# A transformer block on one Trainium2 core: the remainder of every second gate and up block comes from an accumulating transfer

## The chip, the core and the metric

The kernel runs on one of the eight cores of a Trainium2 chip. A core has a matrix engine (TensorE, PE in the profile; its weight loads are listed as PEld), VectorE (DVE), ScalarE (ACT), GpSimd (POOL) and SyncE (SP), which run their own instruction streams and wait for one another by semaphores, and 16 DMA engines that move data between memory (HBM) and the on-chip buffer (SBUF) or inside SBUF. TensorE adds up in PSUM, a separate memory of 8 banks per partition. The metric is the time of one execution on the device, in microseconds (us).

## The reference

One encoder layer for 256 tokens of width 2048, in float32: a layer norm, a wide projection, two kinds of recurrent mixing (gated linear recurrence and retention), an output projection with a residual and a second layer norm, and then the feed-forward part, which is where the change lies:

```
h = layer_norm(DEEPNORM_ALPHA * h + mix, ln1_g[layer], ln1_b[layer])
ff = (jax.nn.silu(h @ w_gate[layer]) * (h @ w_up[layer])) @ w_down[layer]
h = layer_norm(DEEPNORM_ALPHA * h + ff, ln2_g[layer], ln2_b[layer])
```

The gate and up weights are 2048 x 5632 each, the down weight is 5632 x 2048.

## The kernel before

**Products in split form.** TensorE reads float32 operands in a rounded format (fp32r in the profile). To keep accuracy the kernel splits every operand a into a rounded part, hi, and the remainder, lo = a - hi, and adds up the products hi*hi, hi*lo and lo*hi.

**The weight stream.** All weights come as blocks of 128 partitions x 2048 float32 values (1024 KB). `fetch` (L56 to L61) issues the load of one block from SyncE into a tile `raw`, of which there are three (`rawp`, bufs=3). `split_parts` (L71 to L76) then makes the two parts: ScalarE copies `raw` into `whi` with rounding (L75), and VectorE subtracts, `wlo = raw - whi` (L76). There are three pairs of `whi` and `wlo` (`splitp`, bufs=3). So block n can be split once TensorE is done with block n-3, and block n can be loaded once block n-3 has been split. SyncE issues the loads in the order of the blocks, and waits at each until its `raw` tile is free.

**The gate and up stage.** `hidden` (L828) makes two tiles of 128 hidden features, of gate (u = 0) and then of up (u = 1). Each needs one weight block, so that a call uses four blocks, in the order (u, j) = (0,0), (0,1), (1,0), (1,1). `both` (L830) multiplies a block: for each of 16 chunks of the contraction, one product of `whi` with the hi and lo parts of all tokens (512 columns, L838) and one of `wlo` with the hi part (256 columns, L837, or L841 for the first chunk). For the first chunk the product with `whi` comes first. After a block, ScalarE copies one half of the PSUM bank (L850) and VectorE adds the other to it (L851). PSUM has four such banks for these products (`psp`, bufs=4). After two blocks ScalarE and VectorE work on the pair (L855 and L856, or L858, L860 and L861). The stage is in two pieces, hidden tiles 4 to 23 and 24 to 43, with 40 blocks each, and each piece is followed by products with the down weights, whose blocks are split in the same way. The first four hidden tiles are made by another function, which the change leaves alone.

**What sets the order.** Each engine runs its instructions in the order that the tile scheduler wrote when the kernel was built; a waiting instruction holds back all that come behind it on its engine. A tile of a pool is handed out again when its last reader is done.

Of the kernel before, what the change touches and what calls it, by code (L numbers as in the profile page):

```python
# [31 lines left out]

# column offsets of the packed per-feature parameters
C_LB, C_HG, C_RG, C_RB, C_IG, C_IB, C_1G, C_1B = 0, 16, 24, 32, 40, 56, 72, 88
# [4 lines left out]
def encoder_kernel(ctx: ExitStack, tc: tile.TileContext, x, meta, par, rows, w_in, w_out,  # L39
# [13 lines left out]

# [1 line left out]
    def fetch(src, parts=1):  # L55
# [24 lines left out]

# [1 line left out]
    soon, steps = [], deque()  # L82
# [18 lines left out]
    def token_group(blocks, operand, order, evac, split_of=None, halve=False):  # L101
        """[256 tokens] x [512 columns]; a block has 4 chunks of the contraction; order: (token tile, block)

        halve: the second tile goes by column halves at the end; evac(i, ps, half)
        """
        ps = [psp.tile([P, 512], F32, name="pp") for _ in range(2)]
        ws, left, seen = {}, [sum(1 for t, _ in order if t == i) for i in range(2)], [0, 0]
        for i, g in order:
            if g not in ws:
                ws[g] = split_of(g) if split_of else load_block(blocks[g])  # L110
            whi, wlo = ws[g]
            left[i] -= 1
            if halve and i:
                if left[i]:
                    continue
                n = len(ws)
                for half in range(2):
                    ph = psp.tile([P, 512], F32, name="pp")
                    for k in range(4 * n):
                        a_hi, a_lo = operand(i, k)  # L120
                        c = (k % 4) * 512 + half * 256
                        for m, (a, w) in enumerate(((a_hi, 0), (a_hi, 1), (a_lo, 0))):
                            nc.tensor.matmul(ph[:, :256], a, ws[k // 4][w][:, c:c + 256],  # L123
                                             start=(k == 0 and m == 0), stop=(k == 4 * n - 1 and m == 2))
                    evac(i, ph[:, :256], half)
                continue
            for j in range(4):
                k = 4 * g + j
                a_hi, a_lo = operand(i, k)
                for m, (a, w) in enumerate(((a_hi, whi), (a_hi, wlo), (a_lo, whi))):  # L130
                    nc.tensor.matmul(ps[i], a, w[:, j * 512:(j + 1) * 512],  # L131
                                     start=(seen[i] == 0), stop=(left[i] == 0 and j == 3 and m == 2))
                    seen[i] = 1
                if j % 2:
                    tick()
            if left[i] == 0:
                if halve:
                    evac(i, ps[i][:, :256], 0)
                    evac(i, ps[i][:, 256:], 1)
                else:  # L140
                    evac(i, ps[i])
# [7 lines left out]

# [1 line left out]
    prm = cpool.tile([P, NPAR], F32, name="prm")  # L151
# [33 lines left out]

    # lower bounds: softmax over the two rows, first one
    lb = cpool.tile([P, 8], F32, name="lb")
# [14 lines left out]

# [1 line left out]
    def stats_of(xt, st, np_, c0, c1):  # L204
# [3 lines left out]
    def moments(mom, rstd, shift, st, np_):  # L208
        """mean and variance; 1 / deviation; -mean / deviation"""
        nc.vector.bn_aggr(out=mom[:np_], in_=st[:np_])  # L210
        rsqrt(rstd[:np_], mom[:np_, 1:2], 1, np_, LN_EPS)
        nc.vector.tensor_scalar(out=shift[:np_], in0=mom[:np_, 0:1], scalar1=rstd[:np_], scalar2=-1.0,
                                op0=ALU.mult, op1=ALU.mult)
# [4 lines left out]
    def affine_split(pt, pool, cg, cb, c, hs, ls, on_act):  # L218
        """four transposed [P, P] chunks in PSUM -> scaled, shifted, split"""
        fl = pool.tile([P, 4, P], F32, name="fl", tag="w", bufs=6 if pool is not lnp else 3)  # L220
# [86 lines left out]
    def project(n):  # L307
        """weights stationary: [P features, n tokens]"""
        nonlocal nblk
# [13 lines left out]
    def silu_group(order, dst, scale, split_of=None):  # L323
        """silu of 512 columns, token-major"""
        nonlocal nblk
        b0 = nblk
        nblk += 4

        def evac(i, ps):
            sg = qp.tile([P, 512], F32, name="sg", bufs=2)  # L330
            nc.scalar.activation(sg, ps, AF.Sigmoid)
            nc.vector.scalar_tensor_tensor(out=dst[:, i, :], in0=ps, scalar=scale, in1=sg,
                                           op0=ALU.mult, op1=ALU.mult)
        token_group([w_in[b0 + g] for g in range(4)], halves(xhi, xlo), order, evac, split_of)
# [10 lines left out]
    with tc.tile_pool(name="att", bufs=1) as att:  # L345
# [5 lines left out]
        nc.sync.dma_start(dt, dtab)  # L351
        # retention scores by key tile: [256 queries], [128 + 128 queries], [16 keys, 128 queries]
        RS = att.tile([P, 640], F32, name="RS")
# [3 lines left out]
        def values(ps, v, vm, j, o, om):  # L357
            """feature-major [P, T] in PSUM -> token-major, tiles from column o and 16 tokens from column om"""
            vt = att.tile([P, T], F32, name="vt", bufs=2)
# [10 lines left out]

# [1 line left out]
        W = 2 * SEQ + 2 * NM  # L372

        def hgrn(pr, qt, get_g):
# [28 lines left out]

            # Decays to block boundaries, block sizes b = 1, 2, 4, ...: queries hold the decay from the start of
            # their block, keys the decay to the end of theirs, D the decay over a block.
            E = att.tile([P, 3, 4 * 64], F32, name="E")
# [4 lines left out]
            def across(t, b, w, q):  # L411
                """to blocks of 2 b: odd blocks of queries (q) or even blocks of keys take their neighbour's decay"""
                dv = state["d"][:, :w // b].rearrange("p (n two) -> p n two", two=2)
# [17 lines left out]
            def scores():  # L431
                """keys against the three sets of queries in E, 64 of each tile"""
                scs = []
# [8 lines left out]
            def targets(o, b):  # L442
                """the columns of S of odd and even blocks, two tiles"""
                return [S[:, o:o + 2, :].rearrange("p c (n two b) -> p c n two b", two=2, b=b)[:, :, :, x, :]
                        for x in (1, 0)]
# [8 lines left out]
            def prepare(b):  # L454
                """E: queries of the odd blocks of b; of the odd blocks of 2 b; the latter past one more block"""
                n = 2 * SEQ // (4 * b)
# [61 lines left out]
            def cross():  # L518
                # second tile of queries against the first tile of keys
                sx = pss.tile([P, 512], F32, name="sc")  # L520
# [71 lines left out]

# [1 line left out]
        def retention(r):  # L594
# [18 lines left out]
            def scores():  # L613
                # key tiles: positions 0 .. 127, 128 .. 255, 256 .. 271; queries: positions 16 .. 271
                sc = pss.tile([P, 512], F32, name="sc")
# [69 lines left out]

# [1 line left out]
        acc = actp.tile([P, 2, D], F32, name="acc", tag="big", bufs=2)  # L687
# [40 lines left out]

# [1 line left out]
    ffp = ctx.enter_context(tc.tile_pool(name="ffp", bufs=1))  # L730
# [42 lines left out]

# [1 line left out]
    def h_op(i, k):  # L775
# [24 lines left out]
    def first_hidden():  # L800
        """four hidden tiles, tokens stationary, so that the first tile of tokens can go ahead"""
        gate = [None, None]
# [25 lines left out]
    def hidden(f, s):  # L828
        """two hidden tiles, weights stationary, both parts of the tokens moving at once"""
        def both(u, j):  # L830
            hi, lo = load_block(w_gu[2 * f + 2 * u + j])
            hi = hi.rearrange("p (k c) -> p k c", k=KC)
# [91 lines left out]
def _layout(x, meta_tokens, ln_in_g, ln_in_b, hg_lower_bounds, w_in, hg_norm_g, ret_norm_g, ret_norm_b,  # L924
# [14 lines left out]
    def col_blocks(w):  # L939
        """[feature tile][P rows, chunk x P columns]"""  # L940
        w = a(w)[0].reshape(KC, P, -1, P)
        return w.transpose(2, 1, 0, 3).reshape(-1, P, 2048)

    def row_blocks(w, c0, k0, k1):
        """columns c0 .. c0 + 512, chunks k0 .. k1: [block of 4 chunks][P rows, 4 x 512 columns]"""
        w = a(w)[0][k0 * P:k1 * P, c0:c0 + 512].reshape(-1, 4, P, 512)
# [39 lines left out]
```

## Time and profile before

| | |
|---|---|
| time, median of 2 runs | 1308.49 us (1308.13 to 1308.84) |
| span of the profiled execution | 1308.3 us |
| TensorE busy, share of the span | 1281.8 us, 98% |
| VectorE busy | 755.7 us, 58% |
| ScalarE busy | 541.0 us, 41% |
| GpSimd busy | 12.9 us, 1% |
| DMA engines, mean busy share | 51.5% for the transfers that SyncE issues |
| moved | 237.56 MB, 182 GB/s on average |

The span runs from the first to the last instruction of one execution that the hardware profiler recorded; that is the execution's own time here, and it lies between the two timed runs. Busy shares are averages over stages. Matmuls are pipelined, and their ends in the records are modelled, so that a busy TensorE is not one at its peak; where blocks follow each other, the time per block is read from the distance of the ScalarE copies (L850) that each block releases.

### The profile page before, as it was taken

The numbers are of one execution on the slowest core, as the hardware profiler recorded it, in microseconds if no ns is written. First come the engines' busy times: TensorE is split into PE (matmuls) and PEld (weight loads), VectorE is DVE, ScalarE is ACT, GpSimd is POOL, SyncE is SP. The second block draws the span as 40 slices with busy tenths as digits, with TensorE's granted clock in tenths as the row PEclk, the third lists the DMA queues.
The fourth block names the chain that finished last, engine by engine and source line by source line (L and its number), as shares of the span: only waits on it lengthen the run. The fifth ranks groups of instructions, "written<-read, shape, count | busy, mean of one in ns | idle before, by whom it ended". The sixth has DMA issues, their size and how long they took to land.

```text
span 1308.3 us, 17600 instructions
## 1 busy us (share of the span) xinstructions
PE 1281.8 (98%) x7516; PEld 1125.6 (86%) x7516; DVE 755.7 (58%) x872; ACT 541.0 (41%) x570; POOL 12.9 (1%) x24
## 2 busy tenths in 40 slices
PE   6999999999999999999999999999999999999996
PEld 4989999898999988878888888888888888888886
DVE  7764575565557576675555555544445555555555
ACT  7533334343343333573444444433334444443340
POOL 0000000000000000000000000000000000000000
PEclk9999999999999999999999999999999999999998
DMA  6644443454444477555555555555555555555541
GB/s 230 258 150 151 162 146 126 159 182 149 142 160 147 144 278 269 181 212 188 191 193 184 178 187 191 194 193 193 193 193 186 177 188 191 193 183 189 192 176 65
DMA packets 34958, 237.56 MB, mean 182 GB/s; under 512 B 4016, under 2 KB 4656, under 8 KB 6960
## 3 DMA queue, kind: packets, MB, share of 16 engines
q1 hardware_dynamic: 34880, 236.44, 51.5%
q8 instruction: 59, 0.97, 0.3%
q14 instruction: 19, 0.16, 0.0%
HBM read 234.33 MB, written 2.10 MB: 181 GB/s over the span
## 4 chain that ended last, share of the span: by engine, by line
PE 96%; DVE 2%; ACT 1%; DMA 1%; POOL 0%; issue 0%; SPq 0%; POOLq 0%; DVEq 0%
PE pp L131 32%; PE pp L838 23%; PE pp L317 22%; PE pp L837 11%; PE sc L437 1%; PE pp L123 1%; PE pp L841 1%; DVE wlo L76 1%; PE ms L549 1%; PE sc L618 0%; PE ms L546 0%; DMA xt<-in_x_dram 0%; DMA raw<-in_w_down_dram 0%; ACT fl L225 0%; PE sc L535 0%; ACT whi L75 0%
## 5 line engine op out<-in xcount | busy, mean ns | idle before, releaser
L76 DVE TENSOR_TENSOR wlo<-raw,whi 128x2048 fp32r<-128x2048 f32 (+1 forms) x211 | 479.2, 2271 | 324.1 <-ACT whi L75 317.1
L75 ACT CAST whi<-raw 128x2048 fp32r<-128x2048 f32 (+1 forms) x211 | 399.7, 1894 | 246.0 <-PE pp L131 197.4
L838 PE MATMUL pp<-h,whi 128*128 128x512 f32 x1280 | 446.4, 398 | 0.0
L837 PE MATMUL pp<-h,wlo 128*128 128x256 f32 x1200 | 337.4, 281 | 0.0
L838 PEld LDWEIGHTS pp<-h,whi 128*128 128x128 f32 x1280 | 235.4, 188 | 52.4
L837 PEld LDWEIGHTS pp<-h,wlo 128*128 128x128 f32 x1200 | 226.8, 189 | 3.1
L317 PE MATMUL pp<-xhi,whi 128*128 128x272 f32 (+1 forms) x768 | 224.6, 292 | 0.0
L317 PE MATMUL pp<-xlo,whi 128*128 128x272 f32 (+1 forms) x768 | 219.9, 286 | 0.0
L317 PE MATMUL pp<-xhi,wlo 128*128 128x272 f32 (+1 forms) x768 | 219.2, 285 | 0.0
L131 PE MATMUL pp<-whi,t 128*128 128x512 f32 x648 | 199.6, 389 | 0.0
L317 PEld LDWEIGHTS pp<-xhi,whi 128*128 128x128 f32 x768 | 144.6, 188 | 4.2 <-issue 1.7
L317 PEld LDWEIGHTS pp<-xhi,wlo 128*128 128x128 f32 x768 | 144.7, 188 | 0.2
L317 PEld LDWEIGHTS pp<-xlo,whi 128*128 128x128 f32 x768 | 144.6, 188 | 0.0
L131 PEld LDWEIGHTS pp<-whi,t 128*128 128x128 f32 x648 | 121.6, 188 | 25.1
L850 ACT COPY sum<-pp 128x256 f32<-128x256 f32 x80 | 29.8, 373 | 256.3 <-PE pp L838 256.3
L131 PE MATMUL pp<-wlo,t 128*128 128x512 f32 x324 | 126.2, 389 | 0.7 <-DVE wlo L76 0.7
L851 DVE TENSOR_TENSOR sum<-pp,sum 128x256 f32<-128x256 f32 x80 | 34.0, 425 | 100.8 <-ACT sum L850 100.8
L131 PEld LDWEIGHTS pp<-wlo,t 128*128 128x128 f32 x324 | 60.8, 188 | 13.6 <-DVE wlo L76 0.9
L131 PE MATMUL pp<-whi,xhi 128*128 128x512 f32 x128 | 52.3, 411 | 1.9 <-ACT xhi L229 1.9
L131 PE MATMUL pp<-whi,xlo 128*128 128x512 f32 x128 | 51.0, 398 | 0.8 <-DVE xlo L230 0.8
L131 PE MATMUL pp<-wlo,xhi 128*128 128x512 f32 x128 | 51.5, 402 | 0.0
L131 PE MATMUL pp<-whi,mhi 128*128 128x512 f32 x120 | 46.9, 391 | 0.0
(201 smaller groups left out, 1027.5 us busy)
## 6 DMA issues: line engine op xcount, KB each, us to landing
raw<-in_w_gu_dram SPq DMA_DIRECT2D x88, 1024.0 KB, 4.9
raw<-in_w_in_dram SPq DMA_DIRECT2D x62, 1024.0 KB, 4.9
raw<-in_w_down_dram SPq DMA_DIRECT2D x44, 1024.0 KB, 4.9
raw<-in_w_out_dram SPq DMA_DIRECT2D x16, 1024.0 KB, 4.9
gb<-in_rows_dram SPq DMA_DIRECT2D x6, 1024.0 KB, 7.8
raw<-in_w_in_dram SPq DMA_DIRECT2D x4, 512.0 KB, 8.1
acc<-in_x_dram SPq DMA_DIRECT2D x2, 1024.0 KB, 5.9
out_dram<-acc SPq DMA_DIRECT2D x6, 256.0 KB, 2.3
```

Of the source, the lines that this page charges most:

```text
L75: nc.scalar.copy(hi[:, sl], raw[:, sl])
L76: nc.vector.tensor_tensor(out=lo[:, sl], in0=raw[:, sl], in1=hi[:, sl].bitcast(F32), op=ALU.subtract)
L123: nc.tensor.matmul(ph[:, :256], a, ws[k // 4][w][:, c:c + 256], start=(k == 0 and m == 0), stop=(k == 4 * n - 1 and m == 2))
L131: nc.tensor.matmul(ps[i], a, w[:, j * 512:(j + 1) * 512], start=(seen[i] == 0), stop=(left[i] == 0 and j == 3 and m == 2))
L317: nc.tensor.matmul(ps[:, :n], w[:, kc, :], a[:, kc, T - n:], start=(kc == 0 and j == 0), stop=(kc == KC - 1 and j == 2))
L437: nc.tensor.matmul(sc[:, c * 192:(c + 1) * 192], K[:, (o + c) * P:(o + c + 1) * P], E[:, :, (o + c) * 64:(o + c + 1) * 64], start=True, st ...
L549: nc.tensor.matmul(oo, SM[:NM, j * SEQ + i * P:j * SEQ + (i + 1) * P], Vm[:NM, j, :], start=False, stop=True)
L837: nc.tensor.matmul(ps[:, :SEQ], lo[:, kc, :], h[:, kc, 0, :], start=False, stop=False)
L838: nc.tensor.matmul(ps, hi[:, kc, :], h[:, kc].rearrange("p m t -> p (m t)"), start=(kc == 0), stop=(kc == KC - 1))
L841: nc.tensor.matmul(ps[:, :SEQ], lo[:, kc, :], h[:, kc, 0, :], start=False, stop=False)
L850: nc.scalar.copy(t[:, j, :], ps[:, SEQ:])
L851: nc.vector.tensor_tensor(out=t[:, j, :], in0=ps[:, :SEQ], in1=t[:, j, :], op=ALU.add)
```

## The change

In `hidden`, the second block of each pair (j = 1) is loaded by a new function, `load_added`. ScalarE makes the rounded part as before and also writes minus the rounded block into `wlo`; then a transfer that GpSimd issues reads `raw` and adds it onto `wlo` where it lies, so that `wlo` holds the remainder. There are 40 such blocks. Comments are dropped elsewhere, which moves the lines behind by 9; nothing else is different.

```diff
+    def load_added(src):
+
+        raw, _ = fetch(src)
+        hi, lo = new_split()
+        nc.scalar.copy(hi, raw)
+        nc.scalar.activation(lo, raw, AF.Identity, scale=-1.0)
+        nc.gpsimd.dma_start(lo, raw, accum_op=ALU.add)
+        return hi, lo
...
         def both(u, j):
-            hi, lo = load_block(w_gu[2 * f + 2 * u + j])
+            hi, lo = load_added(w_gu[2 * f + 2 * u + j]) if j else load_block(w_gu[2 * f + 2 * u + j])
```

ScalarE in the middle of the gate and up stage before, for two blocks; L850 is the copy out of PSUM, L75 the rounding copy of the block three further on, L855 belongs to the gate:

```order
L850 COPY sum<-pp 128x256
L75 CAST whi<-raw 128x2048
L850 COPY sum<-pp 128x256
L75 CAST whi<-raw 128x2048
L855 ACTIVATE sg<-sum 128x512
```

ScalarE at the same place now, where L859 is the copy out of PSUM, L85 the rounding copy and L86 the negation of a block with j = 1, and L75 the rounding copy of a block with j = 0:

```order
L86 ACTIVATE wlo<-raw 128x2048
L859 COPY sum<-pp 128x256
L85 CAST whi<-raw 128x2048
L859 COPY sum<-pp 128x256
L75 CAST whi<-raw 128x2048
L864 ACTIVATE sg<-sum 128x512
```

One instruction of 2048 columns is added for two blocks, and it stands ahead of the copy out of PSUM that comes when TensorE is done with the block whose buffers it takes.

GpSimd around the stage now; L193 belongs to the layer norms before and after, L87 is the new transfer:

```order
L193 TENSOR_TENSOR lr<-rst,nhalf 128x1 x2
L87 DMA wlo<-raw 128x2048 x40
L193 TENSOR_TENSOR lr<-rst,nhalf 128x1 x2
```

Between the two norms GpSimd had nothing to do before; now it issues the 40 transfers one after the other, in the order of the blocks.

## Rows read from the trace of the kernel before

**Rows 1.** Page, first line and part 1: busy time, share of the span, instructions

```profile
span 1308.3 us, 17600 instructions
...
PE 1281.8 (98%) x7516; PEld 1125.6 (86%) x7516; DVE 755.7 (58%) x872; ACT 541.0 (41%) x570; POOL 12.9 (1%) x24
```

**Rows 2.** Page, part 4: the chain that ended last, by engine

```profile
PE 96%; DVE 2%; ACT 1%; DMA 1%; POOL 0%; issue 0%; SPq 0%; POOLq 0%; DVEq 0%
```

**Rows 3.** Windows, with the stage's second piece last: columns in the first line

```profile
core 0: us, PE busy (x) PEld busy (x) DVE busy (x) ACT busy (x) POOL busy (x), PEclk, DMA share, GB/s
...
40.00:60.00 20.00, 20.00 (x146) 19.23 (x145) 12.33 (x16) 10.61 (x12) 0.00 (x0) 1.00 0.82 326
...
930.00:1157.00 227.00, 227.00 (x1250) 195.95 (x1249) 124.72 (x101) 94.55 (x91) 0.00 (x0) 1.00 0.54 187
```

**Rows 4.** Timeline of ScalarE, 756 to 804 us: start, duration, engine, line, operation

```profile
762.67 1.91 ACT L75 CAST whi<-raw 128x2048 fp32r<-128x2048 f32 x1
...
768.04 0.37 ACT L850 COPY sum<-pp 128x256 f32<-128x256 f32 x1 [2.95 <-PE pp L838]
768.31 1.91 ACT L75 CAST whi<-raw 128x2048 fp32r<-128x2048 f32 x1
773.69 0.37 ACT L850 COPY sum<-pp 128x256 f32<-128x256 f32 x1 [3.47 <-PE pp L838]
...
779.34 0.37 ACT L850 COPY sum<-pp 128x256 f32<-128x256 f32 x1 [2.94 <-PE pp L838]
```

**Rows 5.** Timeline of VectorE, the same stretch

```profile
763.26 0.69 DVE L858 TENSOR_TENSOR sum<-sum 128x512 f32<-128x512 f32 x1
...
770.26 2.29 DVE L76 TENSOR_TENSOR wlo<-raw,whi 128x2048 fp32r<-128x2048 f32 x1 [1.38 <-ACT whi L75]
```

**Rows 6.** Timeline of TensorE's products, 767.1 to 768.1 us

```profile
767.49 0.28 PE L837 MATMUL pp<-h,wlo 128*128 128x256 f32 x1
```

**Rows 7.** Timeline of TensorE's weight loads, 778.8 to 779.5 us

```profile
779.14 0.19 PEld L841 LDWEIGHTS pp<-h,wlo 128*128 128x128 f32 x1
```

**Rows 8.** Groups of ScalarE by line and shape: busy us, mean ns, idle before

```profile
L75 ACT CAST whi<-raw 128x2048 fp32r<-128x2048 f32 x207 | 395.5, 1910 | 245.6 <-PE pp L131 197.4 <-PE pp L317 33.5 <-issue 10.6
...
L251 ACT ACTIVATE xt<-xt,xs,xr 16x2048 f32<-16x2048 f32 x1 | 2.1, 2082 | 0.0
```

**Rows 9.** Page, part 3: DMA queue, packets, MB, share of 16 engines

```profile
q1 hardware_dynamic: 34880, 236.44, 51.5%
```

**Rows 10.** Page, part 6: loads, count, KB each, us from issue to landing

```profile
raw<-in_w_gu_dram SPq DMA_DIRECT2D x88, 1024.0 KB, 4.9
```

**Rows 11.** Line 59, all loads of weight blocks over the whole span

```profile
DMA to landing us min/median/max: 4.7/4.9/11.5
```

**Rows 12.** What SyncE's queue waited for, 575 to 806 us: total, times, longest

```profile
SPq L59 <- DVE wlo L76: 213.3, 42, 6.4
```

**Rows 13.** Groups of GpSimd by line and shape

```profile
L184 POOL TENSOR_TENSOR lr<-rst,nhalf 128x1 f32<-128x1 f32 x4 | 3.4, 840 | 833.2 <-DVE rst L182 833.2
```

**Rows 14.** Windows of the first products, columns as in Rows 3

```profile
16.00:18.00 2.00, 1.47 (x4) 1.20 (x5) 1.79 (x4) 2.00 (x6) 0.13 (x1) 0.74 0.91 324
18.00:20.00 2.00, 2.00 (x6) 1.54 (x5) 1.54 (x4) 2.00 (x6) 0.42 (x1) 0.50 1.04 430
```

**Rows 15.** Timeline of TensorE at the start, products of 512 columns

```profile
16.53 0.50 PE L131 MATMUL pp<-whi,xlo 128*128 128x512 f32 x1 [0.78 <-DVE xlo L230]
...
18.07 0.63 PE L131 MATMUL pp<-whi,xhi 128*128 128x512 f32 x1
18.49 0.63 PE L131 MATMUL pp<-wlo,xhi 128*128 128x512 f32 x1
...
23.21 0.39 PE L131 MATMUL pp<-whi,xhi 128*128 128x512 f32 x1
23.44 0.40 PE L131 MATMUL pp<-wlo,xhi 128*128 128x512 f32 x1
```

## The prediction

> **What bounds the kernel now.** I read the page's busy times first, then the chain that ended last, then windows of the gate and up stage, then its timeline engine by engine. TensorE is busy for 98% of the span [rows 1], and 96% of the chain that ended last is TensorE's own [rows 2]. In the stage's second piece it is busy for all of 227 us, at full clock, while VectorE works 124.72 us, ScalarE 94.55 us, GpSimd not at all, and the DMA engines have a busy share of 0.54 [rows 3]. So the engine that the change relieves is not the one that sets the time; the question is only whether the new way to the remainder is quick enough.
>
> How quick that is, the timeline tells. TensorE finishes a block every 5.65 us: the PSUM copies start at 768.04, 773.69 and 779.34 us [rows 4]. Take the block that ends at 768.04. VectorE multiplies gate by up one block earlier, at 763.26 [rows 5], which closes a group of four; so this block has j = 0, and its buffers go to the third block after it, which has j = 1 and gets the new treatment. Its rounding copy starts at 768.31 and its remainder is there at 770.26 + 2.29 = 772.55 [rows 4, 5]. TensorE first loads `wlo` of that block at 779.14 [rows 7]. The remainder is 6.6 us early.
>
> **The change part by part.**
>
> *Removed:* 40 subtractions of 2.29 us [rows 5], 92 us of VectorE's time. They are early by 6.6 us and VectorE is half idle, so this is worth 0.
>
> *Added on ScalarE:* 40 negations of 128x2048. The nearest rows are the rounding copy, 1.91 us, and an activation over 2048 columns, 2.08 us [rows 8]; I take 1.91, since it has the same shape, so 76 us in all (at most 83). ScalarE is busy for 42% of the stage [rows 3], so the time fits. The negation stands ahead of the PSUM copy and the rounding copy, which start some 1.7 us later. The rounded part is then there at about 768.31 + 1.7 + 1.91 = 771.9, still 7 us early, and the PSUM bank of a block isn't needed again until three blocks later. Cost 0; without that cover it would be 1.7 us a pair.
>
> *Added on GpSimd:* 40 transfers issued in order. GpSimd does nothing else in the stage [rows 3], and its next own work, the last norm's at 0.84 us apiece [rows 13], comes after it. Only one transfer is due per pair of blocks, in 11.30 us.
>
> *Moved:* the remainder now comes when the transfer has landed. The negation needs only `wlo` of the block before, whose last product runs 767.49 to 767.77 [rows 6]. It is done at about 767.77 + 1.91 = 769.7, and TensorE wants the result at 779.14. So **the transfer has 9.4 us** from the end of the negation to its landing. Call its time A. If A is over 9.4, TensorE stalls for s at every second block. Between the freeing of the buffers and their next use lies one other block with j = 1, which stalls too and so lengthens the budget by s; hence s = A - 9.4 - s, or **s = (A - 9.4) / 2**, 40 times. Each microsecond of A above 9.4 costs 20 us.
>
> *Behind the wait:* the `raw` tile of a block with j = 1 comes free only when its transfer has landed, and SyncE waits at each load for the tile of three blocks earlier, now mostly for VectorE [rows 12]. So the next load with j = 0, and the one with j = 1 that is queued behind it, are issued together when a transfer has landed. That leaves them on time (they land 4.9 us later [rows 10], and the first has 5.65 us until its split may start), but it puts both into the time of the next transfer.
>
> **What A is.** No row shows a transfer that adds, or one that GpSimd issues; a load of the same 1024 KB takes 4.7 us at least, 4.9 in the median, and 11.5 at worst, in queues [rows 11]. How much of that is the engines' work: the share of 51.5% of 1308.3 us over 236.44 MB [rows 9] is 2.85 us per MB, 2.99 per block of 1.049 MB. In a stretch of high demand, 326 GB/s at a share of 0.82 [rows 3] make 398 GB/s, 2.64 us per block; the most that any stretch shows is 430 GB/s [rows 14], 2.44 us. I take 2.64, because the engines will be in high demand, and 4.9 - 2.64 = 2.26 us as the part that is only delay.
>
> The transfer has to read `raw` and to read the old `wlo`, so I count two passes, 5.28 us. Alone it would take 2.26 + 5.28 = 7.5 us, and would be in time. But the two loads of the pair fall into it, 5.28 us more: A = 2.26 + 5.28 + 5.28 = 12.8 us, s = 1.7 us. That agrees with itself: the pair takes 11.30 + 1.7 = 13.0 us, so that a transfer starts 0.2 us after the one before has landed, just as the loads are issued. Time that GpSimd needs to issue it, which no row prices, lets the loads get ahead by as much and hardly changes A while it is a few us. **Sum: 40 x 1.7 = 68 us; 1308.3 + 68 = 1376 us.** The span lies within the two timed runs and 0.2 us from their median, so nothing is added for that.
>
> On the two passes there is a page to weigh. The Trainium skill, "Collectives: The Full Stack", in the section on the bandwidth ceiling, says that a reducing transfer reads two sources through the same read ring, and gives a measured ratio of 1.93 between copying and reducing rates. By that ratio A would be 0.2 us less and the sum 64 us, 1372 us by estimate; no run here shows it yet.
>
> **Bounds of this case.** With 2.44 us per pass A is (4.9 - 2.44) + 4 x 2.44 = 12.2, 56 us, 1364 us. With 2.99 it is 13.9, 89 us, 1397 us. If only one load gets in the way, A is 10.2 and the cost 16 us, 1324 us. Stalls may also cost clock: at the start, after waits of which the last was 0.78 us, the granted clock is 0.50 at 18 to 20 us, the lower of its two levels (1.2 GHz), and products of 512 columns come every 0.42 us where they later come every 0.23 [rows 14, 15]. A block that lost 1.7 us to this in every pair would lengthen the budget as well, so that half of it shows, 34 us, up to 1432 us. This case's own range is 1324 to 1432 us; chance 0.45.
>
> **The rivals.**
>
> *The transfer is in time (not slower).* If the transfer takes one pass, A is at most 4.9 + 5.28 = 10.2 with both loads in the way, and 7.5 with one; with two passes it is 7.5 when the loads have gone. Below 9.4 the landing doesn't hold back the loads either: they then fall behind the transfer, not into it, so this state too keeps itself up. Time 1308 us. For it: the DMA engines are 46% idle [rows 3]. Against it: a third and a fourth pass per pair take 4 x 2.64 = 10.6 of 11.30 us, with little room. The Trainium skill, "DMA: Bandwidth & Descriptors", in the section on the anatomy of a transfer from GpSimd, gives 2.0 us plus the bytes over 436 GB/s: by estimate 4.4 us for 1 MB and 6.8 us for twice the bytes, which would be this case. Chance 0.26.
>
> *The adding itself is slow.* If reading, adding and writing follow one another, or the transfer is cut into small pieces, it takes three passes or more. With three, A = 2.26 + 7.92 + 5.28 = 15.5, s = 3.0, 122 us, 1430 us. With four, the DMA engines have 6 x 2.64 = 15.8 us of work per pair and become the bound: 40 x 4.5 = 182 us, 1490 us; slower still beyond. For it: nothing in the trace has this kind of work, and loads that only copy set the price above. Against it: nothing either. Chance 0.27, about half of it above 1460 us.
>
> *Faster.* VectorE's 92 us would have to be worth something, and TensorE waits for it nowhere in the stage [rows 3]. Chance 0.02.
>
> **How the numbers follow.** 2% is 26 us, about what a measurement here can tell from no change; it takes A over 10.7 us. The forecast is the likeliest case, 1376 us. The range of 1305 to 1460 us takes in the transfer that is in time, all of the likeliest case and the mild half of the slow adder; some 0.15 is left out. Chances: faster by over 2% 0.02; within 2% the in-time case and a little of the low end of the likeliest, less what of the former is over the line, 0.27; slower by over 2% the rest, 0.71.
>
> **What would show it.** TensorE waiting some 40 times, for 1 to 3 us, before the first product with `wlo` of a block with j = 1, released by the transfer; pairs of PSUM copies (L859) 13.0 us apart instead of 11.30; transfers from L87 landing 12 to 14 us after issue; SyncE's loads issued in twos after a landing; a DMA share above 0.8 in the stage. Negations near 1.91 us and a VectorE that is 92 us less busy would show the free parts right. If TensorE doesn't wait and the transfers land within 9 us, the collision with the loads is wrong; if they take 15 us or more, the two passes are.

## The result, and the profile after

The changed kernel takes 1395.47 us (median of 2 runs, 1389.89 to 1401.04) against 1308.49 us: 1.0661 times the time before, with a 95% interval of 1.0634 to 1.0687. The forecast was 1376 us, with a range of 1305 to 1460 us. The profiled execution has a span of 1399.3 us, 91.0 us more than before.

First the busy times and the chain that ended last, from the page of the changed kernel:

```profile
PE 1308.8 (94%) x7516; PEld 1138.6 (81%) x7516; DVE 664.0 (47%) x832; ACT 614.1 (44%) x610; POOL 47.9 (3%) x64
...
PE 61%; DMA 31%; issue 4%; DVE 2%; ACT 1%; SPq 0%; POOL 0%; POOLq 0%; DVEq 0%; ACTq 0%
```

VectorE is 91.7 us less busy and ScalarE 73.1 us more, as the parts of the change say [rows 1]. What is new is in the chain: the DMA, 1% of it before [rows 2], now holds 31%, by line 16% for loads of gate and up blocks and 15% for the new transfer, so that the loads weigh as much as the transfer. TensorE's busy time has grown by 27.0 us although it runs the same products, to which I come back.

Then the transfers, from parts 3 and 6 of the page: a queue's packets, MB and share of the 16 engines; an issue's count, size, and median us to landing. The last two lines are the shortest, median and longest landing, first of line 87 (GpSimd's issue), then of line 59 (SyncE's loads) from 575 to 870 us, in the stage's first piece:

```profile
q1 hardware_dynamic: 34880, 236.44, 48.8%
q0 software_dynamic: 5760, 41.95, 14.7%
...
raw<-in_w_gu_dram SPq DMA_DIRECT2D x88, 1024.0 KB, 6.3
...
wlo<-raw POOLq DMA_DIRECT2D x40, 1024.0 KB, 12.0
...
DMA to landing us min/median/max: 6.9/12.0/15.1
...
DMA to landing us min/median/max: 4.7/6.4/14.2
```

The transfer that was priced at 12.8 us takes 12.0 in the median. The engines work 14.7% of 1399.3 us / 40 = 5.14 us on each; the prediction had counted 5.28. The loads land later than before, 6.3 us instead of 4.9 [rows 10].

What the engines waited for, from the list of waits (total us, times, longest), TensorE first, then ScalarE's negation, then SyncE's queue:

```profile
PE pp L850 <- DMA wlo<-raw: 65.0, 32, 3.3
...
ACT wlo L86 <- DMA raw<-in_w_gu_dram: 77.3, 18, 5.9
...
SPq L59 <- DVE wlo L76: 566.4, 106, 12.0
SPq L59 <- DMA wlo<-raw: 492.2, 40, 14.8
```

TensorE stalls 32 times at the first product with the remainder (L850), 65.0 us in all, where the prediction had 40 times 1.7 us. But ScalarE's negation also waits, 18 times and up to 5.9 us, for a load, which the prediction had called on time.

The windows of a long stall show the rest (columns as in Rows 3), and with them a stretch of the stage:

```profile
646.00:649.00 3.00, 0.07 (x1) 0.00 (x0) 0.00 (x0) 0.00 (x0) 0.00 (x0) 1.00 0.50 147
649.00:652.00 3.00, 2.85 (x11) 2.47 (x12) 0.42 (x1) 2.63 (x3) 0.43 (x1) 0.67 0.61 175
652.00:655.00 3.00, 3.00 (x15) 2.59 (x14) 0.00 (x0) 1.34 (x1) 0.44 (x1) 0.77 1.04 371
...
720.00:840.00 120.00, 106.63 (x573) 90.38 (x572) 36.48 (x41) 60.15 (x54) 7.83 (x9) 0.96 0.85 230
```

TensorE stands still from 646 to 649 us, and then runs at a mean granted clock of 0.67 and 0.77 of full speed; in the two 3 us stretches it issues 11 and 15 products, where it issues 19 in each 3 us at full clock from 655 to 661 us. How much of the 27.0 us of extra busy time is the clock, the mean granted clock of the whole span tells, before and now, and the first product after the stall shows a second part:

```profile
core 0: 1308.3 us, clock 0.994
...
core 0: 1399.3 us, clock 0.980
...
649.15 0.38 PE L850 MATMUL pp<-h,wlo 128*128 128x256 f32 x1 [3.08 <-DMA wlo<-raw]
```

What is missing to full clock is 0.020 of 1399.3 us now, 28 us, and was 0.006 of 1308.3 us, 8 us: the lowered clock accounts for some 20 of the 27.0 us at most. The first product after a stall takes 0.38 us where one of its kind takes 0.28 us in the stream [rows 6], by estimate 3 us for 32 stalls; the remaining 4 us are not explained. **The account of the 91.0 us: 65.0 us of waiting and 27.0 us of longer busy time, of which at most some 20 are the lowered clock's; the sum is 1 us over.**

### The profile page after: what moved, and what is told of

It is laid out like the page before. It is cut to its first block, busy times and chain, and to the rows that moved or that the text cites. A ratio compares the mean times of both kernels' runs of the same rounds, so it can differ in the third digit from the quotient of the medians.

```text
span 1399.3 us, 17686 instructions
## 1 busy us (share of the span) xinstructions
PE 1308.8 (94%) x7516; PEld 1138.6 (81%) x7516; DVE 664.0 (47%) x832; ACT 614.1 (44%) x610; POOL 47.9 (3%) x64
## 3 DMA queue, kind: packets, MB, share of 16 engines
q0 software_dynamic: 5760, 41.95, 14.7%
## 4 chain that ended last, share of the span: by engine, by line
PE 61%; DMA 31%; issue 4%; DVE 2%; ACT 1%; SPq 0%; POOL 0%; POOLq 0%; DVEq 0%; ACTq 0%
PE pp L140 30%; PE pp L326 21%; DMA raw<-in_w_gu_dram 16%; DMA wlo<-raw 15%; PE pp L847 3%; PE pp L846 1%; PE sc L446 1%; PE pp L132 1%; ACT wlo L86 1%; DVE wlo L76 1%; PE ms L558 0%; DMA prm<-in_par_dram 0%; PE sc L627 0%; PE ms L555 0%; ACT whi L75 0%
## 5 line engine op out<-in xcount | busy, mean ns | idle before, releaser
L76 DVE TENSOR_TENSOR wlo<-raw,whi 128x2048 fp32r<-128x2048 f32 (+1 forms) x171 | 387.3, 2266 | 279.7 <-ACT whi L75 272.7
L847 PE MATMUL pp<-h,whi 128*128 128x512 f32 x1280 | 462.7, 409 | 0.0
L75 ACT CAST whi<-raw 128x2048 fp32r<-128x2048 f32 (+1 forms) x171 | 323.3, 1891 | 249.4 <-PE pp L140 189.6
L846 PE MATMUL pp<-h,wlo 128*128 128x256 f32 x1200 | 345.4, 288 | 0.0
L847 PEld LDWEIGHTS pp<-h,whi 128*128 128x128 f32 x1280 | 244.9, 196 | 54.5
L846 PEld LDWEIGHTS pp<-h,wlo 128*128 128x128 f32 x1200 | 237.0, 198 | 2.1
L86 ACT ACTIVATE wlo<-raw 128x2048 fp32r<-128x2048 f32 x40 | 76.5, 1914 | 129.9 <-DMA raw<-in_w_gu_dram 77.3
L859 ACT COPY sum<-pp 128x256 f32<-128x256 f32 x80 | 29.0, 363 | 140.6 <-PE pp L847 140.6
L850 PE MATMUL pp<-h,wlo 128*128 128x256 f32 x80 | 26.7, 334 | 65.0 <-DMA wlo<-raw 65.0
L850 PEld LDWEIGHTS pp<-h,wlo 128*128 128x128 f32 x80 | 15.5, 193 | 81.0 <-DMA wlo<-raw 78.8
L85 ACT CAST whi<-raw 128x2048 fp32r<-128x2048 f32 x40 | 76.2, 1905 | 0.0
L140 PEld LDWEIGHTS pp<-wlo,t 128*128 128x128 f32 x324 | 60.8, 188 | 12.8 <-DVE wlo L76 0.2
```

The costliest lines, as they stand in the source:

```text
L75: nc.scalar.copy(hi[:, sl], raw[:, sl])
L76: nc.vector.tensor_tensor(out=lo[:, sl], in0=raw[:, sl], in1=hi[:, sl].bitcast(F32), op=ALU.subtract)
L85: nc.scalar.copy(hi, raw)
L86: nc.scalar.activation(lo, raw, AF.Identity, scale=-1.0)
L140: nc.tensor.matmul(ps[i], a, w[:, j * 512:(j + 1) * 512], start=(seen[i] == 0), stop=(left[i] == 0 and j == 3 and m == 2))
L846: nc.tensor.matmul(ps[:, :SEQ], lo[:, kc, :], h[:, kc, 0, :], start=False, stop=False)
```

## The experiments

Unless said otherwise, every time is a median of several runs beside runs of the kernel before on the same chip, and the ratio is against those, with its 95% interval. Line numbers in the diffs' neighbourhood shift with each edit.

**The negation without the transfer.**

```diff
-        nc.gpsimd.dma_start(lo, raw, accum_op=ALU.add)
+        nc.vector.tensor_tensor(out=lo, in0=raw, in1=lo.bitcast(F32), op=ALU.add)
```

> The negation on ScalarE stays, but VectorE adds the block onto it; there is no transfer from GpSimd. Theory (the landing of the transfer is what TensorE waits for, and the rest is free): no stall, 1308 us, within 3 us. Rival (the negation ahead of the PSUM copy is what delays the stage): 1.7 us per pair, 1376 us or more.

1309.19 us, ratio 1.0004 (0.9995 to 1.0013). ScalarE's extra work is free, and its place ahead of the PSUM copy too. All the cost comes with the transfer that takes the addition's place.

**One pass instead of two.**

```diff
-        nc.gpsimd.dma_start(lo, raw, accum_op=ALU.add)
+        nc.gpsimd.dma_start(lo, raw)
```

> The transfer writes the block over the negated one instead of adding it, so one pass over SBUF instead of two (the second block of each pair is then multiplied with the block itself as its remainder). Theory (A is fixed delay plus the transfer's passes plus the loads in its way): A falls from 12.0 to about 9.4 at most, the transfer's engine time from 5.1 to about 2.6 us, and the time is 1308 to 1325 us. Rival (what takes long is that GpSimd issues it): A stays at 11 to 12 us and the time near 1390 us.

1310.81 us, ratio 1.0015 (1.0002 to 1.0027). The queue of GpSimd's transfers and their landing:

```profile
q0 software_dynamic: 5760, 41.95, 8.2%
...
wlo<-raw POOLq DMA_DIRECT2D x40, 1024.0 KB, 5.2
```

8.2% of a span of 1309.4 us / 40 = 2.68 us of the engines, against 5.14 for the adding one: a factor of 1.92. The Trainium skill, "Collectives: The Full Stack", in the section on the bandwidth ceiling, has a measured ratio of 1.93 between the rates of a collective copy and a collective reduction, because the latter reads two sources. These two runs agree, at 1.92. That GpSimd issues the transfer is not what takes long.

**Half of the columns.**

```diff
-        nc.gpsimd.dma_start(lo, raw, accum_op=ALU.add)
+        nc.gpsimd.dma_start(lo[:, :1024], raw[:, :1024], accum_op=ALU.add)
```

> The transfer adds only the first 1024 columns, the other half of the remainder stays minus the block. Theory (adding costs two passes by the bytes, 5.14 us of all 16 engines for the whole block, 2.68 for a plain copy of it): some 2.6 us of the engines per transfer, A near the 5.2 us of the plain copy, 1308 to 1312 us. Rival (adding has a price of its own per transfer): A of 9 us and more, above 1330 us.

1308.43 us, ratio 0.9996 (0.9986 to 1.0005); A is 4.7 us, and the queue's share of 8.4% makes 2.74 us of the engines per transfer. So the price of adding goes by the bytes here, and has no large part per transfer.

**One load for both blocks of a pair.**

```diff
-        raw, _ = fetch(src)
+        raw, _ = fetched
...
-            hi, lo = load_added(w_gu[2 * f + 2 * u + j]) if j else load_block(w_gu[2 * f + 2 * u + j])
+            hi, lo = load_added(fetched) if j else split(fetched)
...
+            fetched = fetch(w_gu[2 * f + 2 * u])
             for j in range(2):
-                ps = both(u, j)
+                ps = both(u, j, fetched)
```

> One load serves both blocks of a pair (the second block of each pair then has the weights of the first); the transfers are all there. Theory (the two loads of a pair fall into the transfer and make it late): with half of the load work, A is 7.5 to 10.2 us and the time 1308 to 1325 us. Rival (the adding transfer takes about 12 us by itself): A stays at 12, s = 1.3, at least 52 us, 1360 us or more.

1308.52 us, ratio 0.9997 (0.9988 to 1.0007).

```profile
wlo<-raw POOLq DMA_DIRECT2D x40, 1024.0 KB, 7.0
```

With half of the loads the same adding transfer lands after 7.0 us instead of 12.0. The prediction had 7.5 us for it alone. The Trainium skill, "DMA: Bandwidth & Descriptors", in the section on the anatomy of a transfer from GpSimd, gives 2.0 us plus the bytes over 436 GB/s, by estimate 6.8 us for the doubled bytes. This run agrees, with 7.0 us, and the changed kernel shows what that sum leaves out, the loads in the way. (One load less also unties the raw tiles, so this run doesn't tell the two apart.)

**Every fourth block.**

```diff
-            hi, lo = load_added(w_gu[2 * f + 2 * u + j]) if j else load_block(w_gu[2 * f + 2 * u + j])
+            hi, lo = load_added(w_gu[2 * f + 2 * u + j]) if j and u else load_block(w_gu[2 * f + 2 * u + j])
```

> Only the blocks (1,1), every fourth, get the transfer: 20 transfers. If each transfer cost the same wherever it stands, half of the 87 us would stay, 1352 us. Theory (a transfer is late only when the loads that the one before it released fall into it): between two transfers there are now 22.6 us, the loads are over before the next begins, A is 7.5 to 9 us, and the time 1308 to 1315 us.

1309.7 us, ratio 1.0003 (0.9994 to 1.0013), and A:

```profile
wlo<-raw POOLq DMA_DIRECT2D x20, 1024.0 KB, 7.1
```

The 20 transfers cost nothing: the cost isn't a price per transfer, it comes with how densely they follow.

**The remainder later.** In blocks with j = 1 the products with the remainder come last.

```diff
+            if j:
+                for kc in range(KC - 1):
+                    nc.tensor.matmul(ps, hi[:, kc, :], h[:, kc].rearrange("p m t -> p (m t)"),
+                                     start=(kc == 0), stop=False)
+                for kc in range(KC):
+                    nc.tensor.matmul(ps[:, :SEQ], lo[:, kc, :], h[:, kc, 0, :], start=False, stop=False)
...
+                nc.tensor.matmul(ps, hi[:, KC - 1, :], h[:, KC - 1].rearrange("p m t -> p (m t)"),
+                                 start=False, stop=True)
+                return ps
```

> In the second block of each pair TensorE makes the products with the remainder last (15 of the 16 products with the rounded part come first), so that the remainder is wanted some 3.5 us later: budget 12.9 us instead of 9.4. Theory (s is half of what A lacks to the budget): with A at 12 to 13 us s is 0 to 0.1, the time 1308 to 1320 us. Rival (the DMA engines are full in the stage, so that a later deadline only moves the stall): above 1350 us. Rival (late loads of the blocks with j = 0 and 1, not the landing, make the stalls): above 1340 us.

1345.2 us, ratio 1.0291 (1.0246 to 1.0336): a miss. The later deadline takes away more than half of the cost, but not all, and the third of the theories named there, late loads, has a part. Three issues of GpSimd, SyncE's next two loads, and ScalarE's rounding copy and negation, from the timeline of this run:

```profile
727.04 0.87 POOL L87 DMA_DIRECT2D wlo<-raw  x1 [15.54 <-ACT sum L870]
735.87 0.87 POOL L87 DMA_DIRECT2D wlo<-raw  x1 [7.96 <-ACT sum L870]
752.59 0.87 POOL L87 DMA_DIRECT2D wlo<-raw  x1 [15.85 <-ACT sum L870]
...
738.09 1.63 SPq L59 DMA_DIRECT2D raw<-in_w_gu_dram  x2
...
747.88 1.91 ACT L75 CAST whi<-raw 128x2048 fp32r<-128x2048 f32 x1 [6.97 <-DMA raw<-in_w_gu_dram]
749.69 0.62 ACT L875 ACTIVATE sg<-sum 128x512 f32<-128x512 f32 x1
750.38 1.92 ACT L86 ACTIVATE wlo<-raw 128x2048 fp32r<-128x2048 f32 x1
```

The load of the third block on can't start before the transfer of 727.04 has landed, since that transfer reads the raw tile which the load needs. The transfer lands after 11.0 us, at 738.0, and the load goes out at 738.09. Its rounding copy waits for it until 747.88, and the negation of the block after stands behind that copy on ScalarE. So the transfer of 752.59 follows from the one of 727.04: 25.55 us for two pairs that have 22.6. This second loop, through the raw tile, runs beside the one in the prediction.

**A fourth raw tile.** The block (1,1) of each call gets a tile of its own, so that a load with j = 0 no longer waits for a landing.

```diff
+    rawx = ctx.enter_context(tc.tile_pool(name="rawx", bufs=1))
...
-            hi, lo = load_added(w_gu[2 * f + 2 * u + j]) if j else load_block(w_gu[2 * f + 2 * u + j])
+            hi, lo = load_added(w_gu[2 * f + 2 * u + j], rawx if u else rawp) if j else load_block(w_gu[2 * f + 2 * u + j])
```

> A fourth raw tile in the gate and up stage (the block (1,1) of each call has a tile of its own), so that a load with j = 0 no longer waits for a landing. Theory 1 (TensorE's wait for the landing is the whole cost, the loads only lengthen A): A stays near 12, the time within 15 us of the changed kernel's 1395 us. Theory 2, from the run with the remainder last (a second loop: negation, transfer, landing frees the raw tile, load, rounding copy of the next block but two, next negation but one; 2.2 + 12.0 + 6.3 + 2.5 = 23.0 us for two pairs that have 22.6): without that loop ScalarE waits for no load, and the time falls to 1330 to 1375 us, where the wait for the landing alone keeps it.

1366.84 us, ratio 1.0442 (1.0417 to 1.0467), as the second theory had it. From its waits:

```profile
ACT wlo L86 <- PE pp L847: 101.9, 38, 3.5
...
PE pp L851 <- DMA wlo<-raw: 43.6, 22, 3.5
```

The negation now waits, 38 times, for TensorE to free its buffer, and no longer for a load. What is left is TensorE's wait for the landing, 43.6 us, and 13.2 us more of busy time than before (1295.0 against 1281.8 us).

**Both remedies together.** The diff is the sum of the last two.

> The fourth raw tile and the remainder last in the second block of each pair, together. Theory 2 (two loops, by the landing that TensorE waits for and by the raw tile, each with a remedy): both are loosened, 1308 to 1320 us. Rival (the DMA engines are full): 1330 us or more, as with the remainder last alone (1345 us).

1319.07 us, ratio 1.0070 (1.0055 to 1.0085). TensorE's wait for the landing, and the negation's wait for a load:

```profile
PE pp L850 <- DMA wlo<-raw: 13.2, 12, 2.6
...
ACT wlo L86 <- DMA raw<-in_w_gu_dram: 48.9, 13, 5.1
```

TensorE's products wait 13.2 us and its weight loads, which come just ahead of them, 18.9 us. The loads are late here too, so the second loop is loosened and not gone.

**Transfers onto a side tile.** VectorE makes every remainder; the same transfers go to a tile nobody reads.

```diff
-        nc.scalar.activation(lo, raw, AF.Identity, scale=-1.0)
-        nc.gpsimd.dma_start(lo, raw, accum_op=ALU.add)
+        nc.vector.tensor_tensor(out=lo, in0=raw, in1=hi.bitcast(F32), op=ALU.subtract)
+        nc.gpsimd.dma_start(scratch, raw, accum_op=ALU.add)
...
+    scratch = xtra.tile([P, 2048], F32R, name="scratch")
```

> VectorE makes all remainders, as in the kernel before, and beside it the same 40 adding transfers go onto a tile that nothing reads. Theory (waits, not the DMA work as such, cost the time): no stall, 1308 to 1315 us, with a DMA share in the stage as high as 0.7 to 0.85. Rival (the load of the DMA engines delays the weight blocks whoever waits for the transfer): 1335 us or more.

1355.11 to 1387.53 us in four runs, 1371.7 us in the profiled one: a miss, and the most instructive one. Even the fastest is 46 us above the kernel before (1308.93 us). Two issues of GpSimd, one of the rounding copies that wait for a load, and ScalarE's waits:

```profile
766.78 0.87 POOL L87 DMA_DIRECT2D scratch<-raw  x1 [13.18 <-DMA scratch<-raw]
781.25 0.87 POOL L87 DMA_DIRECT2D scratch<-raw  x1 [13.60 <-DMA scratch<-raw]
...
780.48 1.91 ACT L85 CAST whi<-raw 128x2048 fp32r<-128x2048 f32 x1 [5.26 <-DMA raw<-in_w_gu_dram]
...
ACT whi L85 <- DMA raw<-in_w_gu_dram: 107.7, 25, 5.3
...
ACT whi L75 <- DMA raw<-in_w_gu_dram: 97.2, 23, 6.5
```

No product needs what these transfers write, but each holds its raw tile, and the one side tile makes each wait for the landing of the one before. So at a landing the next transfer and the two loads that the landing released go out together, and the transfer lands after 13.6 us in the median. That is the collision of the prediction (A of 12.2 to 13.9 us) with no product waiting for the landing. Holding the raw tile is enough to cost 46 us or more in this arrangement; the changed kernel has no side tile, so this is not the raw tile's share there.

**The same without holding a raw tile.** The transfers read tokens in place of the raw block.

```diff
-        nc.gpsimd.dma_start(scratch, raw, accum_op=ALU.add)
+        nc.gpsimd.dma_start(scratch, h.rearrange("p k m t -> p (k m t)")[:, :2048], accum_op=ALU.add)
```

> As with the side tile: VectorE makes all remainders, and 40 adding transfers go onto a tile that nothing reads. But now they read tokens that stay where they are, not the raw block, so that they hold no raw tile; each follows as soon as the one before has landed, about one in 8 to 11 us, closer together than in the changed kernel. Theory (the landing holds a raw tile and the remainder, and these two waits cost the time): 1308 to 1315 us. Rival (the run with the side tile, 1380 us, was slow because the transfers fill the DMA engines and delay the loads): 1340 us or more.

1312.31 us, ratio 1.0028 (1.0018 to 1.0038). Two windows of the stage's first piece, columns as in Rows 3:

```profile
575.00:700.00 125.00, 125.00 (x674) 107.36 (x673) 70.82 (x57) 55.72 (x52) 9.18 (x11) 1.00 0.99 290
700.00:880.00 180.00, 180.00 (x964) 154.45 (x963) 97.89 (x78) 74.57 (x70) 14.37 (x17) 1.00 0.98 283
```

The DMA engines are at a busy share of 0.98 to 0.99, more than in this stage of any other run, and TensorE is busy for every microsecond. The 40 transfers are over by 1023 us, so this holds for the first piece of the stage, 305 us in which the changed kernel's TensorE was idle for 29. Full DMA engines by themselves cost some 4 us here. In the stage, the code differs from the run before only in what the transfers read: what costs is the raw tile that is held while a transfer is under way.

**A budget of some 16 us.** The fourth raw tile, remainder products last for j = 1, and first for j = 0, by this addition:

```diff
+            if not j:
+                for kc in range(KC):
+                    if kc == 0:
+                        nc.tensor.matmul(ps, hi[:, 0, :], h[:, 0].rearrange("p m t -> p (m t)"), start=True, stop=False)
+                    nc.tensor.matmul(ps[:, :SEQ], lo[:, kc, :], h[:, kc, 0, :], start=False, stop=False)
+                for kc in range(1, KC):
+                    nc.tensor.matmul(ps, hi[:, kc, :], h[:, kc].rearrange("p m t -> p (m t)"),
+                                     start=False, stop=(kc == KC - 1))
...
+                return ps
```

> The fourth raw tile, the products with the remainder last in blocks with j = 1, and first in blocks with j = 0, so that their wlo comes free some 3.5 us earlier: a budget of 16.4 us instead of 9.4. Theory (two loops, the second still there through the loads): from 1319 us, where TensorE still waited 19 us for landings, to 1308 to 1314 us. Rival (what is left there is the order of the products): 1319 us or more.

1300.55 us, ratio 0.9935 (0.9920 to 0.9951): TensorE no longer waits for a landing although the transfers take 10.2 us in the median, and the kernel is faster than the one before, below the 1308 to 1314 us of the theory. Three PSUM copies from its timeline:

```profile
748.41 0.37 ACT L882 COPY sum<-pp 128x256 f32<-128x256 f32 x1 [2.87 <-PE pp L864]
...
759.52 0.37 ACT L882 COPY sum<-pp 128x256 f32<-128x256 f32 x1 [3.37 <-PE pp L864]
...
770.62 0.37 ACT L882 COPY sum<-pp 128x256 f32<-128x256 f32 x1 [2.91 <-PE pp L864]
```

A pair takes 11.11 us instead of 11.30 [rows 4].

**That order in the kernel before.** The two additions for the order of the products, with VectorE's remainders and three raw tiles.

> The kernel before, all remainders from VectorE, three raw tiles, with the order of the products of the last run (remainder products first in blocks with j = 0, last in blocks with j = 1). Theory (what that run gained on the kernel before is the order of the products: its pairs of PSUM copies are 11.10 us apart instead of 11.30, and 40 x 0.20 = 8 us): 1301 us, within 2 us, with no transfer at all. Rival (the gain needs VectorE to be relieved): 1309 us.

1301.82 us, ratio 0.9946 (0.9932 to 0.9959).

```profile
744.23 0.37 ACT L872 COPY sum<-pp 128x256 f32<-128x256 f32 x1 [2.87 <-PE pp L841]
749.77 0.37 ACT L872 COPY sum<-pp 128x256 f32<-128x256 f32 x1 [3.37 <-PE pp L854]
755.33 0.37 ACT L872 COPY sum<-pp 128x256 f32<-128x256 f32 x1 [2.85 <-PE pp L841]
```

Again 11.10 us for a pair, and no transfer at all. The gain is the order of the products; the intervals of the two runs overlap, so no gain from the transfer is shown.

## Why the prediction was right, and where it wasn't

The direction, the place and the mechanism held; the time came out 19 us above the forecast. Against the sum's 68 us of waiting stand 65.0 us, and beside them 27.0 us of longer busy time that the sum didn't have. That the waiting comes out so near is partly luck, as the third point shows.

- *The removed and added work is free.* Shown: the negation without the transfer changes nothing, and VectorE's 92 us are worth nothing, since with half of the columns VectorE is relieved as much (664.3 us busy) and the time is 1308.43 us.
- *A = 12.8 us.* Measured 12.0. The two passes of adding are shown (5.14 us of the engines against 2.68 for a copy), and so is the fixed part with them: 7.0 and 7.1 us with few loads in the way, predicted 7.5. That the rest is the loads, the trace of the changed kernel shows by itself, when issues and landings are laid side by side: 37 of its transfers meet two loads that are under way, and land after 12.1 us in the mean; the three that meet one land after 8.1 us. The side tile agrees, where transfer and two loads start together and A is 13.6 us.
- *s = (A - 9.4) / 2, 68 us.* TensorE waits 65.0 us for the landing. From a landing of 12.0 us and the 0.3 us that lie between the negation's end and GpSimd's issue the formula gives 1.45 us and 58 us. So the shorter landing takes 10 us off the 68, and something else adds 7 to the 58. The even rhythm, 13.0 us for each pair, isn't what happens. The issues of L87 in the changed kernel:

```profile
745.51 0.87 POOL L87 DMA_DIRECT2D wlo<-raw  x1 [14.50 <-ACT sum L859]
756.80 0.87 POOL L87 DMA_DIRECT2D wlo<-raw  x1 [10.42 <-ACT sum L859]
773.03 0.87 POOL L87 DMA_DIRECT2D wlo<-raw  x1 [15.36 <-ACT sum L859]
784.27 0.87 POOL L87 DMA_DIRECT2D wlo<-raw  x1 [10.37 <-ACT sum L859]
799.93 0.87 POOL L87 DMA_DIRECT2D wlo<-raw  x1 [14.79 <-ACT sum L859]
```

Short and long intervals take turns here, 11.3 and 16.2 us, 11.2 and 15.7 us; over the stage's second piece the mean is (1258.79 - 998.84) / 19 = 13.7 us. In most of the long ones the negation, or the rounding copy that stands ahead of it on ScalarE, waits for a load, as ahead of the issues of 745.51 and 773.03:

```profile
740.86 1.90 ACT L75 CAST whi<-raw 128x2048 fp32r<-128x2048 f32 x1 [2.52 <-DMA raw<-in_w_gu_dram]
...
770.82 1.92 ACT L86 ACTIVATE wlo<-raw 128x2048 fp32r<-128x2048 f32 x1 [5.37 <-DMA raw<-in_w_gu_dram]
```

Not in all: ahead of the issue of 799.93 the negation waits last for TensorE, 0.51 us, which has been held up by a landing.

- *"That leaves them on time" failed.* The prediction let the landing hold back the loads and then called the loads punctual, because they land 4.9 us after issue. They land 6.3 us after issue in the median, and the second of two far later, for the same reason that the transfer is late: the load that the negation of 770.82 waits for goes out at 757.19, 0.4 us behind a transfer (756.80), and lands 13.5 us later. So there is a second loop through the loads: landing, raw tile, load, rounding copy, next negation. With a fourth raw tile the time falls from 1395 to 1367 us; with the later deadline alone to 1345; with both to 1319. Each loop alone keeps the stall up, so each remedy alone gets part of it.
- *The clock.* It stood among the bounds, with up to 34 us for the likeliest case, and not in the sum. TensorE's busy time grew by 27.0 us, at most some 20 of them by the clock. The stalls are longer and rarer than the even 1.7 us of the prediction, up to 3.3 us; why some stalls lower the clock and others don't was not tried.
- *The rivals.* "In time" is the state of the runs with half of the transfers or half of the loads, where all takes 1308 to 1310 us. "The adding itself is slow" is excluded by the engines' time, 1.92 times that of a copy, and by the half block. That full DMA engines are enough to hold up the weights is excluded by the transfers that hold no raw tile. Left open is whether the lowered clock comes from the length of the stalls or from their number: with the fourth raw tile TensorE's wait falls by 21.4 us and its busy time by 13.8 us (1308.8 to 1295.0), both at once.

## What to carry to other kernels

A transfer that takes the place of an engine's instruction needs its time compared with two things: with the moment that its result is wanted, and with the moment that its source is wanted back. Both are loops through buffers, and at their edge the transfer's landing releases just the loads that make the next one late. Where such a loop is short of time, look first for order: products that need the late operand can go last, and those that free its buffer first, here some 6 us of budget for nothing (15.9 us instead of 9.4: in the run with both orders a negation can end at 752.4 us, and its remainder is first wanted at 768.3), and with it a kernel that is half a percent faster than the one before.

## What the runs showed that was not expected

- Loads in the way lengthen a plain copy too: in the run with one pass, the 14 copies that meet two loads land after 9.1 us in the mean, the 26 that meet one after 4.9 us.
- With the DMA engines at a share of 0.98 to 0.99 and 283 to 290 GB/s, a weight stream of 187 GB/s [rows 3] still came in time over 305 us, as long as the transfers held no raw tile.
- With 16 products of 256 columns in a row and up to 30 of 512, in place of the two kinds in turn, a pair of blocks takes 11.10 us instead of 11.30. Which pairing of weight load and product makes the difference wasn't tried.
